# Queries and keys of four heads in one wide unit, and another bank, tile and order for retention's first heads

## The chip, the cores and the metric

The kernel runs on one core of a Trainium2 chip. The metric is the time of one execution in microseconds on the device; the profiled execution has a trace of every engine beside it.

## What is computed

Two layers on x of 512 rows and 2048 columns, all in float32. The first is forgetting attention with 16 heads of 128; the second is retention with 8 heads of 256 (queries, keys) and 512 (values). Each ends in a layer norm over `ALPHA * x + branch`. Cut to the part that the change touches:

```python
q, k, v, gate, f_logit = split(x @ w_in)          # 2048 columns each, and 16
q = rms_norm(heads(q), q_gain); k = rms_norm(heads(k), k_gain)
c = cumsum(log_sigmoid(f_logit + b_f))
p = softmax(causal(q @ k.T * scale + c[:, None] - c[None, :]))
y = ((p @ v) * silu(gate)) @ w_out                # first layer
q, k = rotary(q), rotary(k) * 256 ** -0.5         # second layer
o = group_norm(chunkwise_retention(q, k, v)); y = (o * silu(gate)) @ w_out
```

## The kernel before

**Products.** Every float32 product is made of three: each operand is split into a high part (ScalarE copies it into the rounded form, line 305) and a low part (VectorE subtracts, line 306), and `mm3` multiplies high by high, high by low and low by high (lines 310 to 312). On top of that each projection is a Strassen-like scheme with seven half-size products p1 to p7 instead of eight. A `Unit` is one such projection of a group of columns: *narrow* units (two times 256 columns, 256 wide matmuls) make queries and keys of one pair of heads in the first layer or one head in the second, *wide* units (two times 512 columns, 512 wide matmuls) make gate and value of four heads in the first layer or of one head in the second. A `Plain` is the same without the scheme, in eight products. A unit's seven products are cut into blocks: two blocks a product in a narrow unit, four in a wide one. One block is 24 narrow matmuls or 12 wide ones, and needs one split of a weight tile of 128x1024 and sometimes an add before it (lines 570 and 575).

**Order of the blocks.** `ORDER` interleaves p1 with p5, then p6, then p3 with p7, then p2 with p4, whose raw quarter of the weights is shared. `blocks_of` writes this out.

**Accumulators and kept sums.** A unit takes three accumulator banks x, y, z of b0, b1, b2 in turns. When p1, p5 or p6 is complete, `keep` copies the bank into an SBUF tile (line 423), later products are added to it (lines 458, 463, 468), and `hand` gives the finished quarter to the unit's sink. In a wide unit p1 is kept in k0, p5 in k1, the sum of p6 in k2; the gate's first half stays in k0 until it is used. In retention's head 1, p5 of the wide unit is kept in y0, and the narrow unit keeps its sums in y0 and k1.

**The planner.** `Order` writes all engines' instructions in one order by hand. One block is one slot: weights are loaded up to nine blocks ahead (SP's queue), added three blocks and split two blocks ahead. Between blocks, tasks (attention of a head, norms, stores) put in a step each, if their rings of tiles have room and if VectorE's and ScalarE's planned debts stay under `LIMIT`; a slot pays back its planned length. `require` breaks this: if a block needs a tile or bank that is not yet free, all tasks are stepped by force until it is.

```python
LIMIT = 4.4, 3.8
        self.time = 2.72 if self.line[i].u.wide else 2.88
            if not forced and any(d + c > most and c for d, c, most in zip(self.debt, cost, self.most)):
                continue
```

**First layer.** Pair 0 is a `Plain`, then come gate and value of heads 0 to 3, and then narrow units for pairs 1 to 6 with a wide one for gate and value after pairs 1, 3 and 5; pair 7 is a `Plain`. `Pair.take` copies the four finished quarters of queries and keys into the raw tiles in0 and in1 (line 994) and squares each head (line 999); `normed` waits for all four, scales by the root mean square, transposes, applies the gains, and frees in0 and in1. `head` then runs one head of attention, in eight steps.

**Retention.** Head 0's queries and keys are a `Plain` whose two row halves (`EACH[0]`, `EACH[1]`) use one bank; `take_qk` copies them out (line 1576) when in0 and in1 are free. Between the two halves stand p2 and p1 of its wide unit, after them p5, p6, p3 with p7, and p4. `attend` rotates queries and keys (lines 1609 to 1616) and makes the decayed scores; `retain` multiplies by the values, norms each chunk (from line 1720), scales the gates by it (line 1753), transposes (line 1740) and stores y and -y (lines 1744, 1745). After the third scaling it gives back the gate's first half.

Of the kernel before, what the change touches and what calls it, by code (L numbers as in the profile page):

```python
# [11 lines left out]
F32 = mybir.dt.float32  # L12
# [5 lines left out]
P = 128  # L18
# [34 lines left out]
FIRST = (("p2",), ("p1",))  # L53
REST = (("p5",), ("p6",), ("p3", "p7"), ("p4",))
ORDER = (("p1", "+p5"), ("p6",), ("p3", "p7"), ("p2", "p4"))

EARLY = (("p1",), ("p5",), ("p2", "p6"), ("p3",), ("p7",), ("p4",))

# [29 lines left out]
class Order:  # L88
# [17 lines left out]
    def give(self, ring, after=0):  # L106
        if after:
            self.later.append((self.now + after, ring))
        else:
            self.free[ring] += 1  # L110
# [7 lines left out]
    def spawn(self, steps, rank=2):  # L118

        task = dict(steps=steps, last=self.now - 1, rank=rank)  # L120
        try:
            task["need"] = next(steps)
        except StopIteration:
            return
        at = sum(t["rank"] <= rank for t in self.tasks)
        self.tasks.insert(at, task)
# [99 lines left out]
def need(dve=0.0, act=0.0, pe=0.0, wait=1, until=lambda: True, **rings):  # L226
    return dict(dve=dve, act=act, pe=pe, wait=wait, until=until, rings=rings)
# [3 lines left out]
def trunk(ctx: ExitStack, tc: tile.TileContext, xq, x, fb_f, columns, wf_in, narrow, wide, ln_g, ln_b, rot, decay,  # L231
# [676 lines left out]
            split_form("a" + q, aq[q][:, k[0]:k[1]], *k)  # L908
        there.add((q, c))

    fox = dict(heads=0, norms=0)

    def forget():

# [57 lines left out]
    class Pair:  # L972


        def __init__(self, i):
            self.i = i
            self.raw = None
            self.have = self.scored = 0

            self.quick = i >= 6  # L980

            self.tags = HOME["s2"] if i == 7 else ("g0", "g1")
            spare = HOME["s1"][0], HOME["s4"][0]
            self.room = {6: (("d0", "g2"), spare), 7: (HOME["a11"], ("d0", "g2"))}.get(i, [("d0", "g2")] * 2)

        def take(self, m, n, tile, done):
            def copy():
                yield need(act=0.5, until=lambda: self.raw or free["in0"] and free["in1"])
                if self.raw is None:
                    take("in0")  # L990
                    take("in1")
                    self.raw = [pool.tile([P, 2, 512], F32, name="qk_raw", tag=f"in{i}") for i in range(2)]
                    self.ss = pool.tile([P, ST, 4], F32, name="rms_ss", tag="rms_ss", bufs=2)
                nc.scalar.activation(self.raw[m][:, :, n * 256:(n + 1) * 256], tile, AF.Copy)
                yield need(act=1.2)
                for e in range(2):
                    for h in range(2):
                        v = tile[:, e, h * P:(h + 1) * P]
                        nc.scalar.activation(v, v, AF.Square, accum_out=self.ss[:, 2 * m + e, 2 * n + h:2 * n + h + 1])
                done()  # L1000
                self.have += 1

            spawn(copy(), 0)

        def normed(self):

            yield need(until=lambda: self.have == 4 and fox["norms"] == self.i)
            raw = [self.raw[s // 2][:, s % 2] for s in range(ST)]
            r = self.ss
            yield need(dve=1.2)  # L1010
            yield from rsqrt_steps(*[r.rearrange("p a b -> p (a b)")] * 2, 4 * ST, 1.0 / P, QK_EPS)
            for s in range(ST):
                yield need(dve=0.6, wait=0)
                v = raw[s].rearrange("p (h d) -> p h d", h=4)
                nc.vector.tensor_mul(v, v, r[:, s, :, None].to_broadcast([P, 4, P]))
            yield need(until=lambda: all(free[t] for t in self.tags))
            for t in self.tags:
                take(t)
            self.qk = sb8("qk_h", self.tags[0], F32R), sb8("qk_l", self.tags[1], F32R)

            def to_parts(t, s):
                for i, gain in ((0, gq), (2, gk)):
                    h, l = (p[:, i:i + 2, s * P:(s + 1) * P] for p in self.qk)
                    nc.scalar.activation(h, t[:, i:i + 2], AF.Copy, scale=gain)
                    nc.vector.scalar_tensor_tensor(l, t[:, i:i + 2], gain, f32(h), op0=ALU.mult, op1=ALU.subtract)
                give("mmp")

            t, s, last = {}, ST if self.quick else 0, None
            for q in range(ST if self.quick else 0):
                yield need(act=0.75, dve=0.7, pe=0.45, wait=1 - q % 2, mmp=1)  # L1030
                t[q] = by4(mmp())
                for h in range(4):
                    nc.tensor.transpose(t[q][:, h], raw[q][:, h * P:(h + 1) * P], ident)
                to_parts(t[q], q)
            while s < ST or last is not None:
                yield need(act=0.75, dve=0.7, pe=0.45, until=lambda: last is not None or free["mmp"])
                new = None
                if s < ST and free["mmp"]:
                    new = s
                    t[s] = by4(mmp())  # L1040
                    for h in range(4):
                        nc.tensor.transpose(t[s][:, h], raw[s][:, h * P:(h + 1) * P], ident)
                    s += 1
                if last is not None:
                    to_parts(t[last], last)
                last = new
            give("in0")
            give("in1")
            yield need()
            fox["norms"] = self.i + 1  # L1050

# [221 lines left out]
        return sink  # L1273

    pairs = [Pair(i) for i in range(8)]
    qk = [Unit(narrow, i, p.take) for i, p in enumerate(pairs)]
    vg = [Unit(wide, g, gate_and_value(g), u2="k2") for g in range(4)]

    new_quarters(0)
# [14 lines left out]
            ahead[i], before[i] = partial(load_x, *part), partial(split_x, *part)  # L1294
    first.run(BOTH, then={len(BOTH) - 1: lambda: (spawn(forget()), core(0))}, before=before, ahead=ahead)
    vg[0].run(FIRST + REST)
    for i in range(1, 7):
        qk[i].run(then={"p4": partial(core, i), **({"p7": lambda: other_homes()} if i == 6 else {})})
        if i in (1, 3, 5):
            vg[(i + 1) // 2].run()  # L1300

    def fetch(name, *tags):
        for c in (0, 4):
# [3 lines left out]
    def other_homes():  # L1307

        for q in ("11", "12", "22"):
            forms["x" + q], ready["x" + q] = forms["a" + q], set(range(8))  # L1310
        ready["a11"] = ready["a21"] = set()
        home.update(x21=home["s3"], a11=(HOME["s1"][1], HOME["s4"][1]), s1=(HOME["s1"][0], HOME["a11"][0]),
                    s4=(HOME["s4"][0], HOME["a11"][1]))

        def again():

            for c in range(2):
                tags = "k2", "k0", "k1"
                yield need(until=lambda: any(free[t] for t in tags))
                tag = next(t for t in tags if free[t])  # L1320
                take(tag)
                t = pool.tile([P, 4, 256], F32, name="x_raw", tag=tag)
                nc.sync.dma_start(t.rearrange("p a b -> p (a b)"), xq[1, 0, c])
                yield need(dve=1.14, act=0.97, wait=3)
                if c == 0:
                    new_form("x21")
                split_form("x21", t, 4 * c, 4 * c + 4)
                give(tag)
            spawn(fetch("a11", "k2", "k0", "k1"))

        spawn(again(), 1)
# [10 lines left out]
    def two_banks():  # L1342
# [1 line left out]
        banks[:] = c, a, b  # L1344
        return a, b

    Plain(narrow, 7, pairs[7].take, two_banks, kind="x").run(
        BOTH, then={len(BOTH) // 2 - 1: lambda: spawn(fetch("a21", "k2", "k0", "k1")), len(BOTH) - 1: late})


# [189 lines left out]
    class Head:  # L1540
        def __init__(self, h):
            self.h = h
            self.raw = self.v = None
            self.ends = [], []
            self.have = self.have_v = self.have_g = 0
            self.gates = {}
            self.attended = False
            if h == 0:
                self.qk_unit = Plain(narrow, 8, self.take_qk, lambda: [banks[0]] * 2, rows=False)
            else:  # L1550
                self.qk_unit = Unit(narrow, 8 + h, self.take_qk, rows=False, u2="y0")
                if h == 1:

                    self.qk_unit.u2, self.qk_unit.p15_tag = "k1", "y0"
            self.vg_unit = Unit(wide, 6 + h, self.take_vg, u2="k2")
            if h == 1:
                self.vg_unit.p5 = "y0"

        def take_qk(self, m, n, tile, done):

# [223 lines left out]
    for h in heads[1:]:  # L1784
        if h.h == 2:
            spawn(biases())
        h.qk_unit.run(then={"p3": lambda h=h: spawn(h.attend())})
        then = fetch_while(1) if h.h == RH - 1 else {}
        last = then.get("p4", lambda: None)
        h.vg_unit.run(leaves=h.h == RH - 1,  # L1790
                      then={**then, "p4": lambda h=h, last=last: (spawn(h.retain()), last())})


# [141 lines left out]
```

## Time and profile before

| | us |
|---|---|
| median of three runs (lowest, highest) | 2405.23 (2400.59, 2405.72) |
| the profiled execution, its own time | 2403.45 |
| its span, first to last instruction | 2401.7 |
| TensorE busy in it | 2320.4 |
| VectorE, ScalarE, GpSimd busy | 1894.4, 1216.2, 160.7 |
| mean granted TensorE clock | 0.988 |

The span lacks 1.75 us of the execution's own time. Busy time of TensorE counts pipelined matmuls, whose ends are modelled; where the text needs a pace, it takes the steps from start to start. A row of a stretch gives PE, PEld (weight loads), DVE, ACT and POOL in this order.

### The profile page before, as it was taken

What the parts mean: (1) busy time and instruction counts of PE and PEld (TensorE: products, weight loads), DVE (VectorE), ACT (ScalarE), POOL (GpSimd) and SP (SyncE); (2) the same over time, 40 slices, a digit from 0 to 9 for tenths busy, and PEclk for the clock granted to TensorE, in tenths of its full rate; (3) what the DMA queues carried; (4) which work ended last, traced back from release to release, by engine and by line L of the source; (5) the groups of instructions that cost most, each with busy time, mean ns of one, the idle gap of its engine ahead of it and who ended that gap; (6) DMA issues with size and microseconds to landing.
All of it is one profiled execution on the core that took longest, in us unless ns stands there. A gap on an engine that the chain in (4) does not pass through costs nothing.

```text
span 2401.7 us, 34231 instructions
## 1 busy us (share of the span) xinstructions
PE 2320.4 (97%) x13096; PEld 2014.9 (84%) x13096; DVE 1894.4 (79%) x2483; ACT 1216.2 (51%) x1774; POOL 160.7 (7%) x248
## 2 busy tenths in 40 slices
PE   9999999999999999989899999999999999999995
PEld 9888798798799778878779898888889898777784
DVE  5888778678765656679878888898888889987977
ACT  4556556556555534555354545454544445544533
POOL 0000000000000000010020101010101001011002
PEclk9999999999999999999999999999999999999998
DMA  6355544554544467675575857675665659689778
GB/s 225 123 199 175 164 162 159 175 180 153 185 150 156 134 205 233 221 174 154 175 219 194 246 183 220 206 195 187 209 199 193 210 172 265 211 268 292 242 244 190
DMA packets 184564, 471.16 MB, mean 196 GB/s; under 512 B 17968, under 2 KB 63168, under 8 KB 183888
## 3 DMA queue, kind: packets, MB, share of 16 engines
q1 hardware_dynamic: 159136, 395.29, 49.9%
q0 software_dynamic: 25264, 73.69, 12.2%
q8 instruction: 103, 1.69, 0.3%
q14 instruction: 61, 0.50, 0.1%
HBM read 411.20 MB, written 61.91 MB: 197 GB/s over the span
## 4 chain that ended last, share of the span: by engine, by line
PE 44%; DVE 5%; DMA 3%; issue 2%; ACT 1%; POOL 0%; ACTq 0%; DVEq 0%; POOLq 0%
PE acc L310 13%; PE acc L311 13%; PE acc L312 13%; DVE w_l L306 2%; DMA w_raw<-in_wide 2%; PE mmp L310 1%; PE mmp L311 1%; PE mmp L312 1%; DVE w_q L575 1%; ACT w_h L305 1%; PE mmp L1740 0%; DVE z L1840 0%; DMA y_s<-ny 0%; DMA y_s<-y 0%; DMA z_half<-z_in 0%
## 5 line engine op out<-in xcount | busy, mean ns | idle before, releaser
L305 ACT ACTIVATE w_h<-w_q 128x1024 fp32r<-128x1024 f32 x360 | 380.4, 1059 | 425.5 <-DVE w_q L575 218.3
L310 PE MATMUL acc<-w_h,a 128*128 128x512 f32 (+1 forms) x1536 | 551.4, 359 | 6.2 <-DVE kept L468 3.5
L311 PE MATMUL acc<-w_l,a 128*128 128x512 f32 (+1 forms) x1536 | 545.3, 355 | 1.8 <-DVE w_l L306 1.8
L306 DVE TENSOR_TENSOR w_l<-w_raw,w_h 128x1024 fp32r<-128x1024 f32 x314 | 383.4, 1222 | 206.2 <-ACT w_h L305 205.3
L312 PE MATMUL acc<-w_h,a 128*128 128x512 f32 (+1 forms) x1536 | 545.1, 355 | 0.0
L306 DVE TENSOR_TENSOR w_l<-w_q,w_h 128x1024 fp32r<-128x1024 f32 x360 | 439.3, 1221 | 118.1 <-ACT w_h L305 111.1
L310 PE MATMUL acc<-w_h,s 128*128 128x512 f32 (+1 forms) x1408 | 515.9, 366 | 4.3 <-ACT qk_raw L1576 2.1
L311 PE MATMUL acc<-w_l,s 128*128 128x512 f32 (+1 forms) x1408 | 512.0, 364 | 8.0 <-DVE w_l L306 7.9
L312 PE MATMUL acc<-w_h,s 128*128 128x512 f32 (+1 forms) x1408 | 510.1, 362 | 0.0
L305 ACT ACTIVATE w_h<-w_raw 128x1024 fp32r<-128x1024 f32 x314 | 331.7, 1058 | 346.7 <-PE acc L312 161.5
L310 PEld LDWEIGHTS acc<-w_h,a 128*128 128x128 f32 x1536 | 290.9, 189 | 48.3 <-issue 7.4
L311 PEld LDWEIGHTS acc<-w_l,a 128*128 128x128 f32 x1536 | 291.0, 189 | 42.5 <-DVE w_l L306 4.8
L312 PEld LDWEIGHTS acc<-w_h,a 128*128 128x128 f32 x1536 | 290.8, 189 | 41.2
L311 PEld LDWEIGHTS acc<-w_l,s 128*128 128x128 f32 x1408 | 267.6, 190 | 51.4 <-DVE w_l L306 13.6
L310 PEld LDWEIGHTS acc<-w_h,s 128*128 128x128 f32 x1408 | 267.5, 190 | 44.1 <-ACT w_h L305 3.0
L312 PEld LDWEIGHTS acc<-w_h,s 128*128 128x128 f32 x1408 | 267.4, 190 | 41.2
L575 DVE TENSOR_TENSOR w_q<-w_q,w_raw 128x1024 f32<-128x1024 f32 x216 | 263.2, 1220 | 9.0 <-DMA w_raw<-in_wide 6.5
L310 PE MATMUL acc<-a,w_h 128*128 128x256 f32 x464 | 132.9, 287 | 4.3 <-ACT qk_raw L1576 3.1
L312 PE MATMUL acc<-a,w_l 128*128 128x256 f32 x464 | 132.7, 286 | 0.8 <-DVE w_l L306 0.8
L311 PE MATMUL acc<-a,w_h 128*128 128x256 f32 x464 | 132.5, 286 | 0.0
L312 PE MATMUL acc<-s,w_l 128*128 128x256 f32 x448 | 126.8, 283 | 0.0
L311 PE MATMUL acc<-s,w_h 128*128 128x256 f32 x448 | 126.7, 283 | 0.0
(231 smaller groups left out, 2976.3 us busy)
## 6 DMA issues: line engine op xcount, KB each, us to landing
w_raw<-in_wide SPq DMA_DIRECT2D x321, 512.0 KB, 4.0
w_raw<-in_narrow SPq DMA_DIRECT2D x144, 512.0 KB, 3.7
w_q<-in_wide SPq DMA_DIRECT2D x64, 512.0 KB, 4.6
room<-in_wide SPq DMA_DIRECT2D x47, 512.0 KB, 5.0
w_q<-in_narrow SPq DMA_DIRECT2D x26, 512.0 KB, 4.0
y_s<-ny POOLq DMA_DIRECT2D x48, 256.0 KB, 7.0
y_s<-y POOLq DMA_DIRECT2D x40, 256.0 KB, 5.9
room<-in_narrow SPq DMA_DIRECT2D x18, 512.0 KB, 4.5
```

The source lines that it names most:

```text
L305: nc.scalar.activation(h, src, AF.Copy)
L306: nc.vector.tensor_sub(l, src, f32(h))
L310: nc.tensor.matmul(ps, a[0], b[0], start=start, stop=False, skip_group_check=True)
L311: nc.tensor.matmul(ps, a[0], b[1], start=False, stop=False, skip_group_check=True)
L312: nc.tensor.matmul(ps, a[1], b[0], start=False, stop=stop, skip_group_check=True)
L575: nc.vector.tensor_add(u.chain[c], u.chain[c], t)
```

## The change

Pairs 1 and 2, and pairs 3 and 4, get one wide unit each: 512 columns of queries and 512 of keys. `take_both` copies the first pair's half of each finished quarter to the raw tiles as before, squares both halves, and stores the second pair's half in DRAM straight from the kept tile (the last one by way of a temporary tile, since it lies in a bank). `fetch` loads the second pair's raw tiles when the first pair's are free. The order is now pair 0, gate and value, pairs 1 and 2, gate and value, pairs 3 and 4, gate and value, pair 5, gate and value, pair 6, pair 7. In retention, head 0's two row halves use two banks, head 1's wide unit keeps p5 in k1, and its blocks run in a new order `SLOW`: p1, p2 and p5 interleaved, then p6, p3 with p7, and p4 alone.

```diff
+SLOW = (("p1", "p2", "+p5"), ("p6",), ("p3", "p7"), ("p4",))
...
         def take(self, m, n, tile, done):
             def copy():
-                yield need(act=0.5, until=lambda: self.raw or free["in0"] and free["in1"])
+                yield need(act=0.5, until=self.has_room)
...
+        def has_room(self):
+            return self.raw or fox["emptied"] == self.i and free["in0"] and free["in1"]
...
+        def squares(self, m, n, tile, at):
+            for e in range(2):
+                for h in range(2):
+                    v = tile[:, e, at + h * P:at + (h + 1) * P]
+                    nc.scalar.activation(tile[:, e, h * P:(h + 1) * P], v, AF.Square,
+                                         accum_out=self.ss[:, 2 * m + e, 2 * n + h:2 * n + h + 1])
+
+        def take_both(self, other, m, n, tile, done):
+            def copy():
+                yield need(act=0.5, until=self.has_room)
+                if self.raw is None:
+                    self.new_raw()
+                    self.new_sums()
+                    other.new_sums()
+                    other.parked = [dram.tile([P, 2, 512], F32, name=f"qk_raw{other.i}{i}") for i in range(2)]
+                nc.scalar.activation(self.raw[m][:, :, n * 256:(n + 1) * 256], tile[:, :, :256], AF.Copy)
+                to = other.parked[m][:, :, n * 256:(n + 1) * 256]
+                last = (m, n) == (1, 0)
+                if last:
+                    yield need(act=0.5, tmp=1)
+                    t = tmp("qk_park").rearrange("p (e n) -> p e n", e=2)
+                    nc.scalar.activation(t, tile[:, :, 256:], AF.Copy)
+                    nc.gpsimd.dma_start(to, t)
+                    give("tmp", 3)
+                yield need(act=1.2)
+                self.squares(m, n, tile, 0)
+                self.have += 1
+                yield need(act=1.2)
+                other.squares(m, n, tile, 256)
+                if last:
+                    done()
+                else:
+                    nc.gpsimd.dma_start(to, tile[:, :, 256:])
+                    done(3)
+                other.stored += 1
+
+            spawn(copy(), 0)
+
+        def fetch(self):
+            yield need(until=lambda: self.stored == 4 and self.has_room())
+            self.new_raw()
+            for t, d in zip(self.raw, self.parked):
+                nc.sync.dma_start(t, d)
+            yield need(wait=4)
+            self.have = 4
...
             give("in0")
             give("in1")
+            fox["emptied"] = self.i + 1
...
-    qk = [Unit(narrow, i, p.take) for i, p in enumerate(pairs)]
+    qk = {i: Unit(narrow, 1 + j, pairs[i].take) for j, i in enumerate((5, 6))}
+    both = {i: Unit(wide, 18 + j, partial(pairs[i].take_both, pairs[i + 1]), u2="k2") for j, i in enumerate((1, 3))}
...
-    for i in range(1, 7):
-        qk[i].run(then={"p4": partial(core, i), **({"p7": lambda: other_homes()} if i == 6 else {})})
-        if i in (1, 3, 5):
-            vg[(i + 1) // 2].run()
+    for i in (1, 3):
+        both[i].run(then={"p4": lambda i=i: (core(i), spawn(pairs[i + 1].fetch()), core(i + 1))})
+        vg[(i + 1) // 2].run()
+    qk[5].run(then={"p4": partial(core, 5)})
+    vg[3].run()
+    qk[6].run(then={"p4": partial(core, 6), "p7": lambda: other_homes()})
...
-                self.qk_unit = Plain(narrow, 8, self.take_qk, lambda: [banks[0]] * 2, rows=False)
+                self.qk_unit = Plain(narrow, 4, self.take_qk, lambda: [banks[0], banks[2]], rows=False)
...
-            if h == 1:
-                self.vg_unit.p5 = "y0"
...
-        h.vg_unit.run(leaves=h.h == RH - 1,
+        h.vg_unit.run(SLOW if h.h == 1 else ORDER, leaves=h.h == RH - 1,
```

The weights of the pairs are laid out to match, on the host.

## Rows read from the trace of the kernel before

**Rows 1.** The page's busy time of each engine.

```profile
PE 2320.4 (97%) x13096; PEld 2014.9 (84%) x13096; DVE 1894.4 (79%) x2483; ACT 1216.2 (51%) x1774; POOL 160.7 (7%) x248
```

**Rows 2.** First-layer stretches: us, each engine's busy us (count), clock, DMA, GB/s.

```profile
287.09:383.29 96.20, 93.42 (x750) 90.68 (x749) 71.01 (x98) 57.74 (x129) 3.23 (x6) 1.00 0.52 171
383.29:486.34 103.05, 99.00 (x472) 79.56 (x471) 77.43 (x138) 60.61 (x122) 3.23 (x6) 1.00 0.48 153
486.34:572.58 86.24, 86.24 (x709) 85.31 (x708) 67.06 (x80) 49.15 (x103) 3.23 (x6) 1.00 0.55 185
```

**Rows 3.** Retention's units by stretch: head 1 wide, head 2 narrow and wide.

```profile
1170.07:1269.96 99.89, 85.63 (x379) 70.27 (x377) 76.15 (x99) 45.39 (x53) 12.46 (x19) 0.91 0.61 183
1269.96:1317.14 47.18, 47.18 (x368) 45.93 (x366) 41.12 (x69) 18.39 (x21) 1.56 (x3) 1.00 0.58 197
1317.14:1399.56 82.42, 82.36 (x379) 68.17 (x377) 71.47 (x72) 44.27 (x52) 12.34 (x19) 1.00 0.74 228
```

**Rows 4.** Timeline of TensorE, narrow unit: first and last of 27 matmuls.

```profile
499.72 0.28 PE L310 MATMUL acc<-w_h,s 128*128 128x256 f32 x1
...
502.84 0.28 PE L312 MATMUL acc<-w_h,s 128*128 128x256 f32 x1
```

**Rows 5.** Timeline of TensorE, wide unit: first and last of 28 matmuls.

```profile
1389.81 0.39 PE L312 MATMUL acc<-w_h,a 128*128 128x512 f32 x1
...
1395.93 0.39 PE L312 MATMUL acc<-w_h,a 128*128 128x512 f32 x1
```

**Rows 6.** Timeline of TensorE: waits in head 0, and one before it.

```profile
1036.20 0.58 PE L310 MATMUL acc<-a,w_h 128*128 128x256 f32 x1 [3.11 <-ACT qk_raw L1576]
...
1062.82 0.67 PE L310 MATMUL acc<-w_h,s 128*128 128x512 f32 x1 [2.05 <-ACT qk_raw L1576]
...
862.31 0.47 PE L310 MATMUL acc<-w_h,a 128*128 128x512 f32 x1 [1.70 <-DVE z L1412]
```

**Rows 7.** The stretches behind these waits (columns as in rows 2).

```profile
1036.20:1039.00 2.80, 2.79 (x13) 2.80 (x14) 2.80 (x3) 1.50 (x2) 0.00 (x0) 0.50 0.78 247
...
1062.80:1066.00 3.20, 3.18 (x8) 2.51 (x9) 1.39 (x2) 0.00 (x0) 0.87 (x1) 0.53 0.97 169
...
862.02:866.00 3.98, 3.69 (x16) 3.11 (x17) 1.96 (x3) 0.69 (x1) 0.00 (x0) 1.00 0.67 205
```

**Rows 8.** Timeline of VectorE: weights of head 0's second half.

```profile
1033.52 1.22 DVE L306 TENSOR_TENSOR w_l<-w_raw,w_h 128x1024 fp32r<-128x1024 f32 x1
```

**Rows 9.** Timeline of TensorE in head 1's wide unit.

```profile
1191.06 0.65 PE L1740 MATMUL mmp<-ident,kept 128*128 128x128 f32 x4 [1.76 <-ACT kept L1753]
1196.83 1.12 PE L1740 MATMUL mmp<-ident,kept 128*128 128x128 f32 x4 [5.12 <-ACT kept L1753]
1204.72 0.79 PE L310 MATMUL mmp<-qk_h 128*128 128x512 f32 x1 [6.78 <-ACT ny L1745]
```

**Rows 10.** Timeline of ScalarE there: the third scaling, and the keep.

```profile
1204.57 0.71 ACT L1753 ACTIVATE gate<-gate,gn_r 128x512 f32<-128x512 f32 x1
1205.18 1.01 ACT L423 ACTIVATE kept<-acc 128x1024 f32<-128x1024 f32 x1
```

**Rows 11.** Timeline of VectorE there: norm steps and rotation steps.

```profile
1173.70 0.16 DVE L289 TENSOR_SCALAR rsq_h<-gn_mv 128x2 f32<-128x2 f32 x1
...
1192.55 0.68 DVE L1616 TENSOR_TENSOR rope<-rope 128x512 f32<-128x512 f32 x1
```

**Rows 12.** Instructions on kept tiles: the squarings and their sums (ns min/median/max).

```profile
L999 ACT ACTIVATE kept<-kept x72: 291/295/303, 182.0 to 720.0; 128x128 f32<-128x128 f32 x72
L999 ACT ACTIVATION_READ_ACCUMULATOR kept<-kept x72: 185/187/193, 182.2 to 720.2; 128x1 f32 x72
```

**Rows 13.** The page's DMA issues: stores from kept tiles.

```profile
values<-kept POOLq DMA_DIRECT2D x8, 512.0 KB, 7.0
```

**Rows 14.** Timeline of SP's queue: loads that start heads 0 and 3.

```profile
192.10 0.34 SPq L1061 DMA_DIRECT2D cb<-c_rows  x1
...
285.90 0.33 SPq L1061 DMA_DIRECT2D cb<-c_rows  x1
```

More of the change, by code (lines that the diff above doesn't have):

```diff
@@ L909, in split_x @@
         there.add((q, c))
-    fox = dict(heads=0, norms=0)
+    fox = dict(heads=0, norms=0, emptied=0)
     def forget():
@@ L977, in __init__ @@
             self.raw = None
-            self.have = self.scored = 0
+            self.have = self.stored = self.scored = 0
             self.quick = i >= 6
@@ L987, in copy @@
             def copy():
-                yield need(act=0.5, until=lambda: self.raw or free["in0"] and free["in1"])
+                yield need(act=0.5, until=self.has_room)
                 if self.raw is None:
[L990 to L993, printed above, removed]
+                    self.new_raw()
+                    self.new_sums()
                 nc.scalar.activation(self.raw[m][:, :, n * 256:(n + 1) * 256], tile, AF.Copy)
                 yield need(act=1.2)
[L996 to L999, printed above, removed]
+                self.squares(m, n, tile, 0)
                 done()
@@ L1003, in take, with new_raw, new_sums @@
             spawn(copy(), 0)
+        def has_room(self):
+            return self.raw or fox["emptied"] == self.i and free["in0"] and free["in1"]
+        def new_raw(self):
+            take("in0")
+            take("in1")
+            self.raw = [pool.tile([P, 2, 512], F32, name="qk_raw", tag=f"in{i}") for i in range(2)]
+        def new_sums(self):
+            self.ss = pool.tile([P, ST, 4], F32, name="rms_ss", tag="rms_ss", bufs=2)
+        def squares(self, m, n, tile, at):
[4 more added lines that the diff above has]
+                                         accum_out=self.ss[:, 2 * m + e, 2 * n + h:2 * n + h + 1])
@@ new lines, in take_both @@
+        def take_both(self, other, m, n, tile, done):
[3 more added lines that the diff above has]
+                    self.new_raw()
+                    self.new_sums()
+                    other.new_sums()
[10 more added lines that the diff above has]
+                yield need(act=1.2)
+                self.squares(m, n, tile, 0)
+                self.have += 1
[8 more added lines that the diff above has]
+            spawn(copy(), 0)
@@ L1005, in normed @@
+        def fetch(self):
+            yield need(until=lambda: self.stored == 4 and self.has_room())
+            self.new_raw()
+            for t, d in zip(self.raw, self.parked):
+                nc.sync.dma_start(t, d)
+            yield need(wait=4)
+            self.have = 4
         def normed(self):
@@ L1345, in two_banks @@
         return a, b
-    Plain(narrow, 7, pairs[7].take, two_banks, kind="x").run(
+    Plain(narrow, 3, pairs[7].take, two_banks, kind="x").run(
         BOTH, then={len(BOTH) // 2 - 1: lambda: spawn(fetch("a21", "k2", "k0", "k1")), len(BOTH) - 1: late})
@@ L1548, in __init__ @@
             if h == 0:
-                self.qk_unit = Plain(narrow, 8, self.take_qk, lambda: [banks[0]] * 2, rows=False)
+                self.qk_unit = Plain(narrow, 4, self.take_qk, lambda: [banks[0], banks[2]], rows=False)
             else:
-                self.qk_unit = Unit(narrow, 8 + h, self.take_qk, rows=False, u2="y0")
+                self.qk_unit = Unit(narrow, 4 + h, self.take_qk, rows=False, u2="y0")
                 if h == 1:
@@ L1910 @@
     part = lambda w, at, n: w[:, at:at + n]
-    pair = lambda i: side(part(fin, 256 * i, 256), part(fin, D + 256 * i, 256))
-    narrow = [pair(i) for i in range(8)]
+    pair = lambda i, n=256: side(part(fin, 256 * i, n), part(fin, D + 256 * i, n))
+    narrow = [pair(i) for i in (0, 5, 6, 7)]
     narrow += [side(part(rin, D + 256 * h, 256), part(rin, 256 * h, 256)) for h in range(RH)]
@@ L1917 @@
     wide += [part(rout[i * D:(i + 1) * D], 1024 * u, 1024) for i in range(2) for u in range(2)]
+    wide += [pair(i, 512) for i in (1, 3)]
     rot, dec = tables()
```

## The prediction

> **What bounds the kernel now.** I read the page's busy table first: TensorE is busy 97% of the span [rows 1], so the time is nearly the sum of what TensorE has to issue, and an edit pays only if it issues less there or takes a wait from it. Next I cut the trace at the borders of the units (the first matmul of each) and read one row per unit [rows 2, 3]. In the first layer the narrow units run with almost no idle time: of 86.24 us for pairs 4 and 5 TensorE is busy 86.24, the weight loader 85.31. The wide unit before them, 103.05 us with dense attention in it, has 4.05 us of TensorE idle. In retention every pair of units from head 2 on repeats: 47.18 us narrow, 82.42 us wide. Head 1's wide unit takes 99.89 us for the same matmuls, 17.5 us more, with 14.3 us idle and a mean granted clock of 0.91 [rows 3]. That is the one large hole in the kernel. Last I read the engines' timelines around the hole and around head 0 [rows 6 to 11].
>
> **Part 1: the wide units for queries and keys.** A narrow unit has 7 products x 8 k x 2 column halves x 3 = 336 matmuls of 256 columns; a wide one has 336 of 512. Two pairs therefore go from 672 narrow matmuls to 336 wide ones, twice. The timeline gives the pace. 26 steps between narrow matmuls take 3.12 us, so 120 ns each [rows 4]; 27 wide steps take 6.12 us, 226.7 ns [rows 5]. Per wide unit 672 x 0.120 - 336 x 0.2267 = 80.6 - 76.2 = 4.5 us are saved, twice 8.9 us. Why 256 columns take more than half of 512 is seen in the weight loader: 85.31 us for 708 loads is 120 ns each, back to back [rows 2], which is the matmul's own pace. In the wide stage 377 loads fill 68.17 of 82.42 us [rows 3] and the loader is no limit.
>
> The rule that speaks against this term: the Trainium skill (TensorE: Matmul & The Clock Gate, "Wait — 56ns, not 53.3ns?") gives the step between warm matmuls as columns over 2.4 GHz plus about 2.5 ns. By it two narrow steps cost 218.3 ns, a wide one 215.8, and the term would be 2 x 336 x 2.5 ns = 1.7 us. The trace's paces disagree with it in both forms, and more in the narrow one.
>
> What else the part moves, and what covers it:
> - Weights: the same quarters, adds and splits of 128x1024, one of each per block as before. No price.
> - ScalarE: three of four copies into the raw tile fall away for the second pair; the 32 squarings of two pairs (0.295 us, 0.187 more to read the sum [rows 12]) stay, but come in bursts of 8, about 3.9 us, where they came in fours. At the end of the unit two such bursts meet within some four blocks. The planner books 1.2 us for four squarings that take 1.9, so ScalarE may run about 3 us behind there; splits are made two blocks ahead (5.4 us), which hides it unless attention is dense at that point.
> - DMA: per wide unit four stores of 256 KB through POOL's queue and two loads of 512 KB through SP's. Stores of 512 KB from kept tiles land in 7.0 us [rows 13]; POOL is busy 7%. The load stands in SP's queue before weight loads, which are issued up to nine blocks (25 us) ahead, and is issued only after pair i has been normed, many blocks after the last store. Hidden. If it weren't, 7 us for each unit.
> - Waits inside attention: here the trace of before has only neighbours. Pairs 1 and 2 now both start at the border to the next wide unit; pairs 3 and 4 too. TensorE's idle was 2.8 us in the units of pairs 2 and 3, 0 in those of 4 and 5, and 4.05 in a wide unit with dense attention [rows 2]. If both new units idle like the last, 1.3 + 4.05 = 5.3 us are lost; if attention becomes calmer, the 2.8 are won. I take a loss of 2.6, half of the first, since a head's turn comes about every 31 us (three heads between 192.10 and 285.90 [rows 14]) and does not fill the longer stretch.
>
> Part 1: 8.9 - 2.6 = 6.3 us, with ends 3.6 and 11.7.
>
> **Part 2: head 0's two banks.** Both row halves of its queries and keys used one bank. Twice TensorE waits there for the copy out of it: the second half's first matmul comes at 1036.20 after 3.11 us idle, and the next unit's p5, which wants the same bank, at 1062.82 after 2.05 [rows 6]. Both stalls are followed by matmuls at the lower clock level (granted 0.50 and 0.53, that is 1.2 GHz, for about 2.8 and 3.2 us [rows 7]): 13 matmuls at 0.213 instead of 0.120 lose 1.1 us, 8 at 0.427 instead of 0.227 lose 1.6. With the second half in a third bank, which p2 has left by then, neither waits for a copy. The first does not win all: its weights' low part is computed from 1033.52 for 1.22 us [rows 8], so it starts about 1034.75, and of 3.3 us 1.8 are won. Of p5, whose weights are split by then, all 2.2. Does the lower clock still follow the 1.6 us that are left? The nearest row says no: after 1.70 us idle ahead of 862.31 [rows 6] the granted clock is 1.00 [rows 7]. So the 1.1 us are taken as won. Sum 1.8 + 1.1 + 2.2 + 1.6 = 6.7 us; ends 3.8 (nothing at the first) and 8.2 (all of it).
>
> **Part 3: head 1's order and tile.** The 17.5 us go at three places: 1.76, 5.12 and 6.78 us idle ahead of 1191.06, 1196.83 and 1204.72 [rows 9], then lower clock. What is late? p1's sum is to be kept in k0, which still holds head 0's gate; it is released by the third scaling in `retain`. The trace shows that scaling at 1204.57 and the keep right behind it at 1205.18 [rows 10]. So at the end of p1, block 7 of the unit, the kernel's order is written out by force: all pending steps of head 0's norm and of head 1's rotation come at once, without products between, and TensorE waits for them in order. y0 is a second such wait, one block later.
>
> In SLOW p1 ends at block 10 and p5 at block 12 instead of 7 and 8, and those blocks hold less VectorE work: per three blocks three splits and one add (4.56 of the planner's 8.16) against two and one per two (3.42 of 5.44). I replayed the planner's rule by hand (limit 4.4, a block pays back 2.72, split, add and rotation's first step 1.14). For the order of before it gives what VectorE did: first norm steps in blocks 0 and 1, the second group in block 3, rotation steps in 1, 3, 4 and 6, and one norm step still missing at block 7 (the steps lie between 1173.70 and 1192.55 [rows 11]). For SLOW the third scaling falls into block 5 to 7 (needed at 10), the end of rotation, which frees k1, into block 8 to 9 (needed at 12). Both are in time. p2 now starts in block 1 and needs the bank out of which the last quarter of queries and keys is copied at the unit's start; I count no wait for it. SLOW no longer shares p2's quarter with p4, so four loads of 512 KB come on top; at a DMA share of 0.61 [rows 3] they are hidden. VectorE has 76.15 us of work in this unit, 92% of 82.42: it fits, but barely. I take 17.0 of 17.5 us; ends 8.7 (half of the hole stays) and 17.5.
>
> **Sum.** 6.3 + 6.7 + 17.0 = 30.0 us. The profiled execution took 2403.45 us (1.75 around its span), the median of the three runs is 2405.23; the sum gives 2373.5 and 2375.2 on the two. I forecast 2374.
>
> **Rivals.** All by the same sum.
> 1. Head 1 still waits: the replay is off by a few blocks, or `retain`'s steps starve for temporaries. For it: 92% VectorE; against it: three blocks of margin. Half to all of the 17 comes back: 2383 to 2391.
> 2. Part 1's gain goes to ScalarE and attention waits, both units like the worst in the trace, and 3 us of ScalarE delay at each: 8.9 - 5.3 - 6 = -2.4 instead of 6.3, about 2383. Against it: ScalarE is busy 57 to 60% in these units [rows 2].
> 3. The narrow pace isn't a property of the form, so Part 1's first term is 1.7 instead of 8.9: 2381. The Trainium skill's rule above would have it so. Against it: 120 and 227 ns stand in every unit that I looked at.
> 4. Slower: the raw tiles in0 and in1 are late. The second wide unit hands over its first product at block 20, and pair 2 must have been normed by then; likewise pair 4 by block 9 of pair 5's unit. If not, the order is forced as in head 1, at the price of that hole, 17.5 us, at two places: 35 against 30, some 2410. It decides when pair 2 is normed later than about 150 us after pair 1 could start (a gate and value unit of some 100 us and 20 blocks of 2.72). Against it: at 31 us a head [rows 14] pair 1's two heads and a norm of each pair take about 90.
>
> **Chances.** Forecast 0.65 (own range 2366 to 2382), rivals 0.13, 0.12, 0.05, 0.05. By the bounds the sum lies between 16.1 and 37.4, so 2366 is about the low end; some runs lie lower, and 2387 takes in rivals 2 and 3 and half of 1. Range 2365 to 2387. Within 0.2% (4.8 us, about what runs of this kernel differ by) nothing points but a mix of 1 and 2: 0.02. Slower 0.05, faster 0.93.
>
> **What would show it.** Right: the two wide units for pairs 1 to 4 at 76.2 us of pace plus their attention; head 1's wide unit near 82.4 us at clock 1.00; head 0 without the waits for the copies, p5 without a lower clock. Wrong: any TensorE wait on the scaling in `retain`, stalls of over 2 us at the border behind a wide query unit, loads of parked tiles that TensorE waits for, or a pace of the narrow units in other places that has changed.

## The result, and the profile after

The changed kernel takes 2376.91 us in the median of four runs (2374.84 to 2379.24) against 2405.02: a ratio of 0.9887 (95% interval 0.9870 to 0.9904), 28 us less. The forecast was 2374, with a range of 2365 to 2387. The profiled execution took 2375.62 us, with a span of 2373.9, 27.8 less than before.

The page's busy table, in answer to [rows 1]:

```profile
PE 2305.4 (97%) x12424; PEld 1972.5 (83%) x12424; DVE 1893.7 (80%) x2477; ACT 1214.0 (51%) x1762; POOL 166.0 (7%) x256
```

672 matmuls are gone, as they should be: two times 672 narrow ones became two times 336 wide. Where the 27.8 us came from is read from the stretches, cut at the first matmul of each unit. First the first layer's (wide unit of pairs 1 and 2, gate and value, wide unit of pairs 3 and 4, gate and value, pair 5), in answer to [rows 2]; the columns are the same.

```profile
149.28:235.06 85.78, 83.86 (x379) 67.95 (x378) 71.82 (x99) 49.49 (x93) 2.61 (x4) 1.00 0.56 187
235.06:336.82 101.76, 95.80 (x453) 77.02 (x451) 78.80 (x135) 60.21 (x126) 5.03 (x9) 1.00 0.54 176
336.82:430.34 93.52, 92.09 (x427) 74.47 (x425) 67.60 (x89) 53.25 (x109) 5.73 (x11) 1.00 0.54 176
430.34:525.78 95.44, 89.41 (x415) 71.85 (x413) 76.71 (x125) 54.47 (x109) 3.52 (x6) 1.00 0.51 170
525.78:577.26 51.48, 49.47 (x396) 48.07 (x395) 37.97 (x56) 31.20 (x67) 2.18 (x4) 1.00 0.61 195
```

Then retention: head 0's p2 and p1, its second half, its p5 to p4, head 1 narrow and wide, head 2 narrow, in answer to [rows 3, 7].

```profile
1001.72:1029.16 27.44, 25.83 (x120) 19.44 (x118) 13.75 (x17) 18.41 (x32) 3.49 (x4) 1.00 0.74 205
1029.16:1053.48 24.32, 23.38 (x192) 23.17 (x193) 23.69 (x23) 15.95 (x18) 0.87 (x1) 1.00 0.75 238
1053.48:1109.38 55.90, 55.90 (x248) 46.14 (x247) 50.89 (x49) 30.68 (x31) 6.04 (x7) 1.00 0.71 180
1109.38:1159.03 49.65, 49.65 (x385) 48.38 (x384) 41.64 (x50) 19.50 (x23) 0.58 (x1) 1.00 0.50 175
1159.03:1242.78 83.75, 82.88 (x378) 68.03 (x377) 74.74 (x99) 44.13 (x53) 11.81 (x18) 1.00 0.74 237
1242.78:1289.96 47.18, 47.18 (x367) 45.91 (x366) 41.45 (x69) 19.13 (x21) 2.14 (x4) 1.00 0.63 224
```

The same three stretches of head 0 took 30.67, 26.62 and 57.60 us, so 7.2 us are won there; head 1's wide unit took 99.89 and takes 83.75, 16.1 us won. From the gate and value unit behind pair 0 to the output projection the first layer takes 714.1 us instead of 717.7, 3.5 us won by the unrounded rows:

```profile
55.69:773.36 717.67, 700.11 (x4407) 621.43 (x4405) 540.91 (x811) 403.75 (x797) 21.75 (x40) 1.00 0.50 164
55.69:769.83 714.14, 691.68 (x3735) 583.65 (x3733) 541.41 (x805) 401.69 (x785) 27.37 (x48) 1.00 0.51 171
```

(before, then changed). TensorE is busy 8.4 us less there and idle 4.9 us more. The three gains are 26.9 of 27.8 us. The units from head 2 on are what they were.

Two views of the changed kernel answer the question where the waits of heads 0 and 1 went. The timeline of TensorE, in answer to [rows 6]: 0.25 and 0.94 us for the second half's first weights, and p5 directly behind it with no wait.

```profile
1029.16 0.39 PE L312 MATMUL acc<-a,w_h 128*128 128x256 f32 x1 [0.25 <-ACT w_h L307]
1029.38 0.28 PE L313 MATMUL acc<-a,w_h 128*128 128x256 f32 x1
1030.61 0.39 PE L314 MATMUL acc<-a,w_l 128*128 128x256 f32 x1 [0.94 <-DVE w_l L308]
...
1053.39 0.28 PE L314 MATMUL acc<-a,w_l 128*128 128x256 f32 x1
1053.51 0.40 PE L312 MATMUL acc<-w_h,s 128*128 128x512 f32 x1
```

The timeline of ScalarE in head 1's wide unit, in answer to [rows 10]: the scalings in `retain` (now line 1813) and the keep of p1.

```profile
1174.80 0.72 ACT L1813 ACTIVATE gate<-gate,gn_r 128x512 f32<-128x512 f32 x1
...
1188.42 1.03 ACT L425 ACTIVATE kept<-acc 128x1024 f32<-128x1024 f32 x1 [0.40 <-PE acc L314]
```

The third scaling is 13.6 us ahead of the keep, which now waits for nothing but TensorE's own product. Before, they touched.

### The profile page after: what moved, and what is told of

Same layout as the page of the kernel before. It is cut to its first block, busy times and chain, and to the rows that moved or that the text cites. A ratio compares the mean times of both kernels' runs of the same rounds, so it can differ in the third digit from the quotient of the medians.

```text
span 2373.9 us, 32923 instructions
## 1 busy us (share of the span) xinstructions
PE 2305.4 (97%) x12424; PEld 1972.5 (83%) x12424; DVE 1893.7 (80%) x2477; ACT 1214.0 (51%) x1762; POOL 166.0 (7%) x256
## 4 chain that ended last, share of the span: by engine, by line
PE 61%; DVE 7%; DMA 4%; ACT 3%; issue 3%; SPq 0%; POOL 0%; DVEq 0%; ACTq 0%; POOLq 0%
PE acc L312 18%; PE acc L313 18%; PE acc L314 18%; DVE w_l L308 3%; DMA w_raw<-in_wide 2%; ACT w_h L307 2%; PE mmp L312 1%; PE mmp L313 1%; PE mmp L314 1%; DVE w_q L577 1%; PE mmp L1277 1%; DMA v_sum<-in_wide 1%; PE mmp L1800 1%; DMA y_raw<-y_a 0%; PE mmp L1132 0%
## 5 line engine op out<-in xcount | busy, mean ns | idle before, releaser
L312 PE MATMUL acc<-w_h,a 128*128 128x512 f32 (+1 forms) x1440 | 535.5, 372 | 7.3 <-DVE kept L470 5.2
L313 PE MATMUL acc<-w_l,a 128*128 128x512 f32 (+1 forms) x1440 | 528.8, 367 | 5.2 <-DVE w_l L308 5.1
L314 PE MATMUL acc<-w_h,a 128*128 128x512 f32 (+1 forms) x1440 | 528.2, 367 | 0.0
L313 PE MATMUL acc<-w_l,s 128*128 128x512 f32 (+1 forms) x1280 | 487.4, 381 | 9.8 <-DVE w_l L308 9.7
L312 PE MATMUL acc<-w_h,s 128*128 128x512 f32 (+1 forms) x1280 | 490.7, 383 | 0.4 <-ACT w_h L307 0.4
L314 PE MATMUL acc<-w_h,s 128*128 128x512 f32 (+1 forms) x1280 | 485.8, 380 | 0.0
L312 PEld LDWEIGHTS acc<-w_h,a 128*128 128x128 f32 x1440 | 272.0, 189 | 53.8 <-issue 9.6
L313 PEld LDWEIGHTS acc<-w_l,a 128*128 128x128 f32 x1440 | 272.3, 189 | 50.8 <-DVE w_l L308 10.2
L314 PEld LDWEIGHTS acc<-w_h,a 128*128 128x128 f32 x1440 | 271.9, 189 | 44.9
L313 PEld LDWEIGHTS acc<-w_l,s 128*128 128x128 f32 x1280 | 241.1, 188 | 59.7 <-DVE w_l L308 17.5
L314 PEld LDWEIGHTS acc<-w_h,s 128*128 128x128 f32 x1280 | 240.7, 188 | 45.4
L312 PEld LDWEIGHTS acc<-w_h,s 128*128 128x128 f32 x1280 | 241.0, 188 | 43.8 <-ACT w_h L307 0.9
```

What stands on the lines that cost most here:

```text
L312: nc.tensor.matmul(ps, a[0], b[0], start=start, stop=False, skip_group_check=True)
L313: nc.tensor.matmul(ps, a[0], b[1], start=False, stop=False, skip_group_check=True)
L314: nc.tensor.matmul(ps, a[1], b[0], start=False, stop=stop, skip_group_check=True)
```

## The experiments

In all of them the yardstick for part 1 is the stretch from the first matmul of the first gate and value unit to the first of the output projection, called the long stretch here: 717.7 us before, 714.1 changed.

**Each half alone.** e1 takes retention back, e2 the first layer.

```diff
 # e1: the changed kernel with
-Plain(narrow, 4, self.take_qk, lambda: [banks[0], banks[2]], rows=False)
+Plain(narrow, 4, self.take_qk, lambda: [banks[0]] * 2, rows=False)
+            if h == 1: self.vg_unit.p5 = "y0"
-        h.vg_unit.run(SLOW if h.h == 1 else ORDER, ...
+        h.vg_unit.run(...
 # e2: the changed kernel with narrow units 1 to 6 in the order of before
```

> Part 1 alone: wide query and key units, retention as before. If the three parts are independent, the first layer ends at 769.8 us as in the changed kernel, 3.5 us earlier than before, retention keeps both holes (head 1's wide unit 99.9 us) and the time is 3.6 us under before, within 0.2% of it. If the parts help each other (the earlier end shifts something in retention), the gain is over 6 us or there is a loss.

> Parts 2 and 3 alone: first layer as before (it ends at 773.4 us). If they carry the gain by themselves, head 0 is 7.2 us and head 1's wide unit 16.2 us shorter and the time is 23.5 to 24.5 us under before. If a share of that comes from the first layer's new order, less than 20 us.

e1: 2403.18 us in the median of ten runs, ratio 0.9999 (0.9989 to 1.0009). The expected 3.6 us did not come: the interval allows a gain of 2.6 us at most. In its trace the long stretch is 715.5 us, 2.2 less than before, the first layer ends at 772.8 us and not at 769.8, and head 1's hole is there (100.2 us). The rest goes in a part that the edit does not touch. The last 300 us of the program, cut at the same matmul, hold the same instructions:

```profile
2100.12:2401.68 301.56, 271.02 (x1169) 218.51 (x1167) 248.75 (x292) 138.51 (x144) 38.43 (x55) 0.96 0.83 247
2099.14:2404.80 305.66, 272.20 (x1169) 219.31 (x1167) 248.80 (x292) 138.65 (x144) 38.32 (x55) 0.95 0.81 243
```

(before, then e1). In the other traces this part takes 299.9 to 304.7 us, so the time of one execution cannot show a gain of a few us; the stretch that was changed can.

e2: 2381.29 us, ratio 0.9912 (0.9895 to 0.9928), 22.4 us less than before, about 1 us short of the expected 23.5 to 24.5; head 0 (its whole share, 141.8 us before) 134.5, head 1's wide unit 82.6, the long stretch 717.7. So retention carries nearly all. What part 1 adds, 0.5 us alone and 4.4 us with retention, is of the size by which runs differ; that the halves do not help each other fits the intervals, and is not shown.

**Tile or order in head 1.**

```diff
 # e4: tile without order
-        h.vg_unit.run(SLOW if h.h == 1 else ORDER, ...
+        h.vg_unit.run(...
 # e5: order without tile
+            if h == 1: self.vg_unit.p5 = "y0"
```

> The changed kernel with head 1's wide unit in the old order, p5 kept in k1. Theory of the prediction: p1's keep in k0 makes the hole, so it stays: the unit takes 95 us or more, TensorE waits for the scaling in retain. Rival: y0 made it and the tile mends it: 85 us or less.

> The changed kernel with the new order in head 1's wide unit, but p5 kept in y0 as before. Theory: the order alone mends the hole, 82.5 to 85 us for the unit, no wait on the scaling. Rival: the tile is needed: 90 us or more.

With the tile alone the unit takes 99.7 us (2393.33 us for the whole, one execution), and TensorE's waits in it are those of before, to 0.1 us:

```profile
PE mmp L1800 <- ACT kept L1813: 6.9, 2, 5.1
PE mmp L312 <- ACT ny L1805: 6.8, 1, 6.8
PE mmp L1800 <- DVE in L1719: 0.6, 1, 0.6
```

(waits of e4, that unit: total, times, longest). With the order alone it takes 83.2 us and has 0.6 us of waits (2378.05 us, one execution). The order does it; in time the tile does nothing.

**One bank again.**

```diff
 # e3
-Plain(narrow, 4, self.take_qk, lambda: [banks[0], banks[2]], rows=False)
+Plain(narrow, 4, self.take_qk, lambda: [banks[0]] * 2, rows=False)
```

> The changed kernel with head 0's two halves in one bank again. Theory: both waits for the copy come back, 3.1 and 2.1 us, with the lower clock behind them, and the span grows by 7 us. Rival: the gain in head 0 came from elsewhere (the order of the first layer): under 3 us.

Both waits for the copy are back, 5.2 us together and 3.1 the longer:

```profile
PE acc L312 <- ACT qk_raw L1636: 5.2, 2, 3.1
```

Head 0 takes 140.7 us, 6.2 more than changed; the whole takes 2384.56 us in its one execution, and its span grew by 8.9 us where 7 were expected. After the second of these waits the granted clock stayed at 1.00 this time, where it is 0.62 in e1: 56.0 us for p5 to p4 instead of 57.6.

**The pace by itself.**

```diff
 # e6, ahead of everything
+    for w, n in ((P, 512), (P, 256), (64, 256), (64, 512), (P, 384), (P, 128), (P, 256)):
+        for i in range(48):
+            nc.tensor.matmul(warm[:w, :n], pace[:, :w], pace[:, :n], start=True, stop=True, ...)
```

> The changed kernel with 7 stretches of 48 matmuls of constant data put ahead of everything: stationary columns x moving columns 128x512, 128x256, 64x256, 64x512, 128x384, 128x128, 128x256. Theory: the weight loader sets the narrow pace at 120 ns, so half the stationary columns bring 256 moving columns to about 113 ns or less, 512 stay at 227, and 128x128 stays near 110 to 120, not half of 256. Rival (a fixed cost in the matmul itself): 64x256 stays at 120.

The edit costs about 53 us of matmuls ahead of the kernel (2431.26 us, one execution); only their pace is of use. The stretches of 128x512, 128x256, 64x256, 64x512 and 128x128 (stationary x moving columns), from the first matmul of one to about the first of the next:

```profile
7.51:18.42 10.91, 10.91 (x51) 9.03 (x50) 7.35 (x6) 6.38 (x6) 0.00 (x0) 1.00 1.03 409
18.53:24.27 5.74, 5.74 (x49) 5.74 (x48) 0.00 (x0) 0.00 (x0) 0.00 (x0) 1.00 0.25 101
24.28:29.72 5.44, 5.44 (x50) 5.44 (x49) 0.00 (x0) 0.00 (x0) 0.00 (x0) 1.00 0.00 0
29.73:40.75 11.02, 11.02 (x50) 6.49 (x49) 0.00 (x0) 0.00 (x0) 0.00 (x0) 1.00 0.00 1
...
49.11:54.40 5.29, 5.29 (x49) 5.29 (x49) 0.00 (x0) 0.00 (x0) 0.00 (x0) 1.00 0.00 0
```

By 48 each: 227, 120, 113, 230 and 110 ns. (The first row ends 0.11 us early; cut at the next stretch's first matmul, 18.53, it gives 230, while most of its steps are 227.) The two stretches left out, 128x384 and 128x256 again, give 174 and 121. Half the stationary columns take 7 ns from a 256-column step and none from a 512-column one; with half of them two narrow steps (227) cost as much as one wide one. So the 13 ns that part 1 saves per pair of narrow matmuls (2 x 120 less 226.7) go with the stationary columns, and the rival, 120 for 64x256, is out. What differs there in the records is the weight load, 134 ns instead of 190:

```profile
L282 PEld LDWEIGHTS mmp<-pace 128*128 128x128 f32 x240 | 34.4, 190 | 2.1
L282 PEld LDWEIGHTS mmp<-pace 128*64 128x64 f32 x96 | 11.9, 134 | 4.4
```

That it is the loader fits, as forecast. The sign by which the prediction knew it, loads back to back, does not show it by itself: at 64 columns they stand back to back too (5.44 of 5.44 us). By the Trainium skill's rule (TensorE: Matmul & The Clock Gate, "Wait — 56ns, not 53.3ns?") the estimate would be 109 ns for 256 and 216 ns for 512 moving columns; no stretch here shows them.

**The way through DRAM.**

```diff
 # e9: every parked store and every load of the raw tiles twice
+                    nc.gpsimd.dma_start(to, tile[:, :, 256:])
+                nc.sync.dma_start(t, d)
 # e12: every store once more, to another place; loads single
+                    nc.gpsimd.dma_start(again, tile[:, :, 256:])
```

> The changed kernel with every store of a parked quarter and every load of the second pair's raw tiles issued twice. Theory: the way through DRAM is hidden, so the eight units of the first layer behind pair 0 and ahead of the output projection keep their 714 us within 2 us (two executions differ by as much). Rival (the loads in SP's queue or the stores that hold k0, k1 and k2 cost time): 4 us or more longer.

> The changed kernel with each parked quarter stored twice, the second time to a place of its own in DRAM, so that no store or load has to wait for another; the loads stay single. If the bytes and the use of POOL's queue are hidden, the stretch from gate and value of heads 0 to 3 to the output projection stays at 713 to 717 us. If the stores themselves cost time (they hold k0, k1 and k2 longer, or crowd the DMA engines), it is 4 us or more longer, as with everything doubled.

e9 fell on the rival's side: its long stretch is 726.8 us, 12.7 more (2387.20 us for the whole, one execution). But the timeline of SP's queue says that the edit had brought in a wait of its own: each second load stands until the first into the same tile has landed.

```profile
281.40 0.37 SPq L1061 DMA_DIRECT2D qk_raw<-qk_raw  x1
285.74 0.33 SPq L1062 DMA_DIRECT2D qk_raw<-qk_raw  x1
286.16 0.38 SPq L1061 DMA_DIRECT2D qk_raw<-qk_raw  x1
291.07 0.32 SPq L1062 DMA_DIRECT2D qk_raw<-qk_raw  x1
291.48 9.48 SPq L563 DMA_DIRECT2D w_raw<-in_wide  x4
```

The weight loads behind them come 10 us later than the first raw load, and the two units concerned take 108.3 and 102.1 us instead of 101.8 and 95.4. In the changed kernel the two loads are issued within 0.85 us:

```profile
282.11 0.85 SPq L1059 DMA_DIRECT2D qk_raw<-qk_raw  x2
284.79 10.32 SPq L563 DMA_DIRECT2D w_raw<-in_wide  x4
```

e12, which doubles the bytes of the stores without such a wait, has 716.9 us (2381.16 for the whole, one execution) and TensorE's waits in sum 22.5 us, against 22.2 in the changed kernel; where the other 2.8 us come from is told in the last section. The stores are hidden, and the single loads are shown to make no wait in the queue; their bytes alone were not doubled cleanly.

**ScalarE's bookings.**

```diff
 # e7, in take_both
-                yield need(act=1.2)
+                yield need(act=1.9)      (both times)
```

> The changed kernel; the planner books the four squarings at 1.9 us, what they take, instead of 1.2. Theory: ScalarE's late work behind the first wide query unit makes the 2.3 us wait at 248 us, so that wait shrinks by 1.5 us or more and the first layer ends 1.5 to 3 us earlier. Rival: the waits come from the number of attention steps that fall there: no change over 0.7 us.

The 2.3 us wait at 248 us is gone and the unit behind the first wide one takes 97.1 instead of 101.8 us, but the next two take 96.7 and 97.2 instead of 93.5 and 95.4. The long stretch is 713.7 us, the time 2376.23 (one execution). The first half of the theory holds, but the 1.5 to 3 us that were expected did not come: the gain is given back. Attention steps that were put off meet the next units: TensorE has 439 matmuls instead of 453 in the first of these units, and 432 and 426 instead of 427 and 415 in the next two, where a new wait of 2.8 us for `pT` stands at 347 us.

**Other places for the wide units.**

```diff
 # e8: wide units for pairs 2, 3 and 4, 5     # e10: for 1, 2 alone     # e11: for 3, 4 alone
-... for j, i in enumerate((1, 3))}
+... for j, i in enumerate((2, 4))}            # e10: ((1,))            # e11: ((3,))
```

> The wide units take pairs 2 and 3, and 4 and 5, pair 1 stays narrow ahead of them. The same matmuls as in the changed kernel; the attention of two pairs starts one unit later. If the lost 5 us of part 1 hang on where the attention falls, the first layer ends 2 to 5 us earlier or later than 769.8; if they are the price of the wide form, it ends within 1 us of it.

> Only pairs 1 and 2 share a wide unit, pairs 3 to 6 stay narrow as before; retention as changed. Of the saved pace 4.4 us. Theory: the loss sits where two pairs start attention at one border; with one such border half of the 5 us is lost, so the stretch from gate and value of heads 0 to 3 to the output projection takes 715 to 717 us (717.7 before, 714.1 changed). Rival: one of the two borders carries all of the loss: this kernel or the next is at 713 or below.

> Only pairs 3 and 4 share a wide unit, the others stay narrow; retention as changed. Theory: half of the saving and half of the loss, 715 to 717 us for the same stretch. Rival: all of the loss lies at one of the borders: 713 or below here, and 717 or above in the other kernel, or the other way round.

The waits are the sum over the list of TensorE's waits in the long stretch; times in us.

| | wide units | matmul pace saved | TensorE's waits, sum | long stretch | ratio (interval) |
|---|---|---|---|---|---|
| before | 0 | 0 | 17.2 | 717.7 | |
| changed | 2 | 8.9 | 22.2 | 714.1 | 0.9887 (0.9870 to 0.9904) |
| e8 | 2 | 8.9 | 30.4 | 724.2 | 0.9945 (0.9928 to 0.9961) |
| e10 | 1 | 4.5 | 16.3 | 712.4 | 0.9887 (0.9872 to 0.9902) |
| e11 | 1 | 4.5 | 17.1 | 714.4 | 0.9901 (0.9885 to 0.9918) |

717.7 less the pace plus the growth of the waits gives 713.8, 722.0, 712.3 and 713.1: the two columns explain the stretches to 0.3 us for the changed kernel and e10, and to 2.2 and 1.3 for e8 and e11. They leave out the clock: in e11 pair 5's unit takes 52.97 us at a granted 0.97, where it takes 51.48 at 1.00 in the changed kernel.

e8 has the same matmuls and is 10 us longer, beyond the 2 to 5 us that were expected, and 4.3 us more are lost right behind the stretch. So the loss is not a fixed price of the wide form; it goes with where attention falls.

e10 met its rival's number (712.4, at most 713), e11 neither its theory nor its rival. Their sums, which are those of before, do not say that a single wide unit costs no wait. The rows of e10, for the unit behind the wide one, pair 3 and the unit behind it:

```profile
235.46:337.22 101.76, 95.80 (x453) 77.02 (x451) 78.89 (x135) 60.17 (x126) 5.02 (x9) 1.00 0.50 165
337.22:389.22 52.00, 51.16 (x400) 48.90 (x399) 37.94 (x58) 32.46 (x74) 2.17 (x4) 1.00 0.57 193
389.22:481.64 92.42, 92.08 (x437) 75.03 (x436) 72.66 (x113) 52.22 (x97) 4.32 (x8) 1.00 0.51 166
```

TensorE is idle for 5.96 us behind the wide unit, exactly as in the changed kernel, where the same unit had 2.2 before. What makes e10's sum low is that the units after it wait less: 0.84 and 0.34 us here, 2.78 in pairs 2 and 3 and 4.05 in the unit behind them before [rows 2]. In e11 it is alike: 4.5 us behind its wide unit and 2.0 in pair 5's, less elsewhere. So each border costs waits of its own, and the order of the units decides how much is won back; these runs do not part the 5 us further. e10 is the shortest in the trace by 1.7 us; but the changed first layer itself, run again in e1, e3, e4 and e5, takes 713.7 to 716.8 us, so of these rows only e8's stands clear, and e10's time, 2375.46 us, cannot be told from the changed kernel's.

## Why the prediction was right, point by point

- *The bound.* Right: the gains are what TensorE issues less and waits less; nothing moved to another engine but eight stores (GpSimd 160.7 to 166.0 us).
- *Part 1's pace*, 8.9 us: right, by the count of matmuls (TensorE's busy time in the long stretch falls by 8.4); e6 shows that it hangs on the stationary columns.
- *Part 1's waits*, taken as 2.6 us with 5.3 as the bad end: mis-sized. They are 5.0 us (22.2 against 17.2), so part 1 gave 3.5 instead of 6.3, just under its low end of 3.6. The reason for halving the bound (attention does not fill the longer stretch) was wrong: both new borders wait, the unit behind the first wide one 5.96 us instead of 2.20, the unit behind the second 6.03 instead of 4.05. And a cost was not in the sum at all: in other executions of the same first layer (e1, e3, e5) the long stretch is 715.5 to 716.8 us, as the last section shows. Over the changed kernel, e1, e3, e4 and e5 part 1 gave 0.8 to 4.0 us, 2.5 in the mean, so the term was more than twice too large; it is small in the sum of 30.
- *ScalarE behind by some 3 us at the end of the wide unit*: it happened where forecast. TensorE waits 2.3 us from 248.8 us for `pT`, behind two bursts of four squarings; e7 takes that wait away and wins nothing. The end of the last burst, the copy that TensorE wants, and the wait:

```profile
250.18 0.26 ACT L1019 ACTIVATE acc<-acc 128x128 f32<-128x128 f32 x1
...
250.44 0.59 ACT L1155 ACTIVATE pT<-mmp 128x512 f32<-128x512 f32 x1
...
251.09 0.55 PE L1132 MATMUL mmp<-ident,p 128*128 128x128 f32 x3 [2.29 <-ACT pT L1155]
```

- *DMA hidden*: right for the stores (e12); the load in SP's queue is harmless only as long as it does not wait (e9).
- *Part 2*, 6.7 us: measured 7.2, and 6.2 in e3. The second half's first matmul was to win 1.8 of 3.3 us: the gap ahead of it, from start to start, went from 3.49 to 0.64 us, and 1.1 more are lost for the low part, so 1.7. That this fits is partly luck: a start at 1034.75 instead of 1036.20 wins 1.45 us and leaves 1.8, so the term took what is left for what is won. The trace makes up for it, since the first two of its matmuls need only the high part and run before the wait for the low one. The lower clock did not follow: granted 1.00 over the second half and p5.
- *Part 3*, 17.0 us: measured 16.1 in the profile, 17.3 in e2. The third scaling was to fall into blocks 5 to 7 and the rotation to end in 8 or 9; by the count of the unit's own matmuls begun by then, 12 a block, they came in blocks 5 and 8 (after 5.7 and 8.9 blocks), and p1's keep after 10.1. That p1's keep is what forced the order fits all of it (e4 and e5, and the scaling just ahead of the keep). No run frees k0 alone, so k0 as the tile is argued, not shown by itself. y0, the second wait that the prediction named, is no cause by itself: with p5 kept in k1 the hole stays (e4), with p5 in y0 and the new order it is gone (e5).
- *Rivals.* 1 (head 1 still waits) did not come; 2 came in part; 3 is out by e6; 4 did not come: the wide unit of pairs 3 and 4 has 1.4 us of TensorE idle in all (93.52 less 92.09).

## What to carry to other kernels

Where an order is written by hand with tiles in few copies, look for the place at which a copy is demanded before its last user has been issued: one such place cost 17 us here, and moving the demand three blocks later, by issuing other ready products first, was worth more than taking away 672 matmuls. Fewer and wider matmuls save only what the narrow step costs beyond half a wide one (13 ns a pair here), and much of that is lost again if they bunch work of other engines: count the waits as well as the paces, unit by unit, since a sum over many units hides which of them waits. A load that waits holds up the loads issued behind it in its queue (10 us in e9). And a gain of a few us is read from several executions of the stretch, not from one.

## What the runs showed of the hardware

The clock does not fall after every wait of the same length. Behind the wait of 2.3 us at 248 us and that of 2.0 us at 532 us the granted clock was 1.00 in the profile of the changed kernel, and 0.71 and 0.56 in that of e12, with the same waits ahead of them:

```profile
250.90:254.50 3.60, 3.42 (x19) 2.85 (x19) 3.29 (x11) 2.63 (x6) 0.00 (x0) 1.00 0.19 55
534.10:538.00 3.90, 3.79 (x32) 3.82 (x33) 3.90 (x4) 1.31 (x4) 0.54 (x1) 1.00 0.77 245
```

(changed kernel), and e12:

```profile
251.10:254.70 3.60, 3.43 (x13) 2.78 (x14) 3.29 (x11) 2.61 (x6) 0.00 (x0) 0.71 0.18 53
535.60:539.50 3.90, 3.84 (x20) 3.87 (x21) 3.90 (x4) 0.89 (x3) 0.54 (x1) 0.56 0.79 255
```

13 matmuls are issued instead of 19, then 20 instead of 32, in the same time, and the two units take 103.3 and 53.0 us instead of 101.8 and 51.5: 1.5 us each. So a wait of some 2 us has a second price that is paid in some executions and not in others, about 3 us of part 1's gain here. e1, whose time shows no gain, has the longer of the two times in the first of these units (103.3 us) and the shorter in the second.

The wait of 2.6 to 2.8 us at some 128 us (50 us later in e6), ahead of both wide units and alike in all traces, goes both ways too: over the 4 us behind it the granted clock is 0.58 before and 0.57 to 0.69 in e1, e3, e5, e6, e7, e8, e10 and e11, and 1.00 in the changed kernel, e2, e4, e9 and e12. There the lower clock costs no time: the unit takes 93.59 us both before and changed, since with the full clock TensorE waits 0.9 us more further on. So 0.9 of the 5.0 us by which the sum of waits grew is no loss of part 1's units.
